# A decoder layer on one core: the MLP's sums all on VectorE, the norm's root applied to the squared activations, another order of the down passes

## The chip, the core and the metric

The kernel runs on one core of a Trainium2 chip. A core has TensorE (matmuls, PE), VectorE (DVE), ScalarE (ACT), GpSimd (POOL) and SyncE (SP, which issues the DMAs). Each engine takes its instructions strictly in the order of its own list; between engines semaphores hold an instruction back until its inputs are there and its buffer is free. The metric is the device time of one execution in microseconds.

## What is computed

One layer of a decoder trunk with two token mixers (a gated DeltaNet and a sparse attention), then an MLP with a squared ReLU. The change lies behind the mixers:

```python
mix = sigmoid(gate_dn) * (o_dn @ w_proj_dn) + sigmoid(gate_nsa) * (o_ns @ w_proj_nsa)
x = x + mix @ w_out
h2 = rmsnorm(x, norm_mlp)          # x * rsqrt(mean(x * x) + 1e-6) * gain
x = x + square(relu(h2 @ w_up)) @ w_down
```

Sequence and model width are 1024, the MLP's inner width is 4096, all float32.

## The kernel before

Everything is held transposed: a tile is 128 features by 512 tokens (128x512), the 1024 tokens being two halves. A float32 matmul is made of three matmuls on fp32r operands: each operand is split in a high part (a copy on ScalarE) and a low part (a subtraction on VectorE, L186 for `split`, L277 for weights in `parts`), and high times high, high times low and low times high are summed in PSUM. So every weight tile costs a DMA, a ScalarE copy and a VectorE subtraction before TensorE can use it.

The stages after the mixers, in the order of the code:

- **Merge** (`ns_merge`, times 1590 to 1679 us): for 8 blocks of features and both halves, the sparse mixer's projection (24 matmuls) is gated and added to the DeltaNet's gated projection. The weights come through `unit` (L280), two loads of 128x4x128 into the ring `wr` of three buffers, which lives in the permanent pool `wp`. `ns_rows` loads the mixer's rows in `a11`. The sum of the two mixers (L1409) is on GpSimd.
- **Output projection** (`out_proj`, 1679 to about 1768 us): 16 blocks (half, c) of 24 matmuls each, in the order (0,0), (1,0), (0,1), (1,1), (0,2), (1,2), then c = 3 to 7 of half 0 and c = 3 to 7 of half 1 (`CB` = 3). Each block's sum x is written to DRAM, squared on ScalarE and added to `sums[half]` (on GpSimd for half 0).
- **Root of the norm** (`root_rows`, L244): eight matmuls with one column (four, each in two passes) put the sums of squares of 512 tokens on partitions, VectorE and GpSimd (`pow`) make 128x4 roots, VectorE spreads them on a diagonal (L252), and one matmul with ones brings them back as 128x512 in PSUM. The first root is taken after block (1,3), the second two products into the up projection.
- **Norm** (`norm_first`, `norm_second`): x times gain times root, one VectorE operation for each of 16 tiles, then the sums of Strassen-Winograd's scheme (B11, B21, T1 to T4, B22), each split in high and low parts (`parts_of`) and held in the big tiles.
- **Up projection** (`up_prep`, `up_mm`, `up_out`, `up_sums`, about 1768 to 2087 us): 16 row blocks n of seven products p (1 to 7) instead of eight. A product is 12 matmuls of 128x512. `weights_of` forms the weight side (a11, a12, a21, a22 and their sums), `up_mm` adds the products in PSUM and on VectorE (L1590, L1594), `up_out` squares the ReLU, and `up_sums` forms four more sums which go to DRAM (`acd`) as right sides for the down projection. Preparation runs `LEAD` = 4 products ahead.
- **Down projection** (`down_load`, `down_prep`, `down_mm`, 2087 to 2401 us): two passes n; in each the seven products p in the order of `turns[n]`, and within each p the eight inner blocks i, accumulated in four PSUM tiles `DP`. The side comes through `bb` and is split in `ah`, `al`. After i = 7 the four tiles are added to the x tiles `X1`. The p = 6 weights are `tmp` = a22 − a11.

Sums not named otherwise went to GpSimd: the helper `sub` (L1450) has GpSimd as its default engine. In `weights_of` that is a21 + a22 at p = 5 and a12 − tmp at p = 6, in `up_prep` and `down_prep` a11 − a21, in `up_sums` the last two. In the first down pass a11 − a21 of inner block e is issued five products into the p = 2 turn, e at a time:

```python
e = q - J - 5
if 0 <= e < J:
    sub(DW[0, e, "a11"], DW[0, e, "a11"], DW[0, e, "a21"])
```

The code gives the instructions; a scheduler in the tile framework sets the order in which each engine's list holds them. So where an instruction stands on its engine is seen from the built program, and rows of it are shown with the change below. Buffers come in rings (pools `pw`, `p5`, `pe`, `pf`, `pg`, `ph`), and a load waits until the ring's oldest buffer has been read.

Of the kernel before, what the change touches and what calls it, by code (L numbers as in the profile page):

```python
# [20 lines left out]
D = 1024  # L21
# [125 lines left out]
def body(ctx: ExitStack, tc: tile.TileContext, A, out):  # L147
# [74 lines left out]
    for half in range(2):  # L222
# [3 lines left out]
        if half == 0:  # L226
            load_consts(cp, 0)
            cp_raw = [wp.tile([128, 4, 128], F32, name="wr", bufs=3) for _ in range(2)]
            for i in range(2):
                SY.dma_start(cp_raw[i], A["w_cp"][0][:, 4 * i:4 * i + 4])  # L230
# [236 lines left out]
    def cmp_hidden(u, i):  # L467
# [3 lines left out]
        w1 = wp.tile([128, 4, 128], F32, name="wr", bufs=3)  # L471
# [444 lines left out]
    def fill_nb(u):  # L916
# [3 lines left out]
        def prep():  # L920
            for kp in range(4):
                wr = wp.tile([128, 2, 256], F32, name="wr", bufs=3)
# [475 lines left out]
    def ns_merge(c, half):  # L1398
# [10 lines left out]
        GP.tensor_tensor(md, md, th, OP.add)  # L1409
# [12 lines left out]
    x1, sums = [[], []], [None, None]  # L1422
# [3 lines left out]
    def out_proj(half, c):  # L1426
# [23 lines left out]
    def sub(o, a, b, eng=None):  # L1450
        (eng or GP).tensor_tensor(o, a, b, OP.subtract)
# [14 lines left out]
    def norm_second(r):  # L1466
        raw = R["raw"]
        R["T2"], R["T3"] = big(True), big(True)
        b12, b22, t = [], [], []

        def head(j):
            b12.append(t512(PL.p5, "b", 4))
            V.scalar_tensor_tensor(b12[j], x1[1][j], cols[:, 8 + j:9 + j], r, op0=OP.mult, op1=OP.mult)
            sub(raw[:, j], b12[j], raw[:, j], V)
            b22.append(t512(PL.p5, "c", 8))
            V.scalar_tensor_tensor(b22[j], x1[1][4 + j], cols[:, 12 + j:13 + j], r, op0=OP.mult, op1=OP.mult)

        def second(j):
            t.append(t512(PL.p5, "c", 8))
            sub(t[j], b22[j], raw[:, j], V)  # L1480
            parts_of("T2", t[j], j)

        head(0)
        for j in range(4):
            if j < 3:
                head(j + 1)
            second(j)
        yield
        for j in range(4):
# [12 lines left out]
        yield

    def weights_of(blocks, p, home):

        a11, a12, a21, a22 = [blocks.get(b) for b in ("a11", "a12", "a21", "a22")]
        if p == 6:
            t = t512(home, "tmp", 2)
            sub(t, a22, a11, V)
# [3 lines left out]
        if p == 5:  # L1513
            GP.tensor_tensor(a21, a21, a22, OP.add)
# [236 lines left out]
```

## Time and profile before

| | |
|---|---|
| Time, median of 3 runs | 2409.52 us (2408.16 to 2412.6) |
| Time of the profiled execution | 2409.07 us |
| Its span | 2407.3 us |
| PE busy | 2339.8 us (97%) |
| DVE busy | 1563.8 us (65%) |
| ACT busy | 1093.4 us (45%) |
| POOL busy | 569.0 us (24%) |

The profile is of one execution by the hardware profiler. The span runs from the first instruction to the last, so 1.8 us of the profiled execution's time lie outside it. Busy times count instructions, not waits. A tile's name in a row is that of the program without its number (`wl<-a,wh` is a low part wl made of a weight tile and its high part); a row of PE with x2 is two matmuls in one record. The releaser in brackets behind an idle time is the instruction that was the last to be waited for.

### The profile page before, as it was taken

How to read it: one execution, taken by the hardware profiler on the slowest of the kernel's cores; microseconds unless marked ns; L12 is line 12 of the kernel's file. 1: busy time of each engine (PE TensorE's matmuls, PEld its weight loads, DVE VectorE, ACT ScalarE, POOL GpSimd, SP SyncE). 2: the span in 40 equal slices, each digit the busy share in tenths (PEclk: the TensorE clock that was granted, in tenths of full speed). 3: DMA queues.
4: the chain of work that ended last, by engine and by line, in shares of the span. 5: the costliest groups of instructions: out<-in, count | busy, mean ns of one | idle time of the engine just before them, and what ended most of it. 6: DMA issues, size and time to landing. Idle time of an engine off the chain costs nothing. (4 is left out here: it accounts for less than half of the span.)

```text
span 2407.3 us, 44378 instructions
## 1 busy us (share of the span) xinstructions
PE 2339.8 (97%) x16673; PEld 1916.8 (80%) x16673; DVE 1563.8 (65%) x3626; ACT 1093.4 (45%) x2258; POOL 569.0 (24%) x473
## 2 busy tenths in 40 slices
PE   7999999999999999999999999999999999989999
PEld 5887878787878887877777777778878888878887
DVE  6766664747484838348877777643397666596785
ACT  4233343434344444227666766532355555534443
POOL 3132321203231423000010111012145444260320
PEclk9999999999999999999999999999999999999999
DMA  5421313131212221237432422164425443566333
GB/s 176 135 65 56 85 43 94 42 91 44 80 50 82 51 77 50 87 116 179 131 115 72 115 89 73 32 225 161 148 83 172 144 149 136 204 232 225 109 126 102
DMA packets 237510, 267.37 MB, mean 111 GB/s; under 512 B 76976, under 2 KB 128496, under 8 KB 237168
## 3 DMA queue, kind: packets, MB, share of 16 engines
q1 hardware_dynamic: 237296, 264.55, 35.2%
q8 instruction: 131, 2.15, 0.4%
q14 instruction: 83, 0.68, 0.1%
HBM read 190.05 MB, written 72.38 MB: 109 GB/s over the span
## 5 line engine op out<-in xcount | busy, mean ns | idle before, releaser
L177 PE MATMUL g<-hh,wh 128*128 128x512 f32 (+1 forms) x816 | 335.4, 411 | 8.2 <-ACT hh L174 7.3
L177 PE MATMUL g<-hl,wh 128*128 128x512 f32 (+1 forms) x816 | 327.4, 401 | 0.1
L177 PE MATMUL g<-hh,wl 128*128 128x512 f32 (+1 forms) x816 | 323.5, 396 | 0.0
L177 PE MATMUL V<-big,wh 128*128 128x512 f32 x768 | 239.4, 392 | 1.6 <-DVE c L1594 1.6
L186 DVE TENSOR_TENSOR wl<-a,wh 128x512 fp32r<-128x512 f32 x192 | 160.6, 838 | 111.0 <-ACT wh L174 110.9
L174 ACT ACTIVATE wh<-wr 128x512 fp32r<-128x512 f32 x210 | 132.1, 630 | 207.1 <-PE g L177 131.4
L174 ACT ACTIVATE wh<-a 128x512 fp32r<-128x512 f32 x192 | 121.1, 631 | 219.6 <-PE V L177 109.5
L1223 DVE CUSTOM_DVE_ANT_0 junk<-S,cst 128x384 f32<-128x384 f32 (+3 forms) x320 | 168.4, 533 | 56.8 <-PE S L177 52.7
L277 DVE TENSOR_TENSOR wl<-wr,wh 128x512 fp32r<-128x512 f32 x178 | 123.6, 698 | 111.9 <-ACT wh L174 108.4
L177 PEld LDWEIGHTS g<-hh,wh 128*128 128x128 f32 (+1 forms) x816 | 153.6, 188 | 36.2 <-ACT hh L174 7.5
L174 ACT ACTIVATE P<-T 128x512 f32<-128x512 f32 x228 | 134.0, 597 | 100.9 <-PE T L177 88.9
L177 PEld LDWEIGHTS g<-hh,wl 128*128 128x128 f32 (+1 forms) x816 | 153.4, 188 | 29.5 <-issue 0.6
L177 PEld LDWEIGHTS g<-hl,wh 128*128 128x128 f32 (+1 forms) x816 | 153.8, 188 | 26.4 <-DVE hl L324 0.8
L177 PEld LDWEIGHTS V<-big,wh 128*128 128x128 f32 x768 | 144.7, 189 | 32.7 <-ACT c L174 1.2
L177 PE MATMUL V<-big,wl 128*128 128x512 f32 x384 | 150.5, 392 | 3.2 <-DVE wl L186 3.2
L177 PE MATMUL g<-wh,hh 128*128 128x256 f32 x512 | 147.4, 288 | 0.0
L177 PE MATMUL g<-wl,hh 128*128 128x256 f32 x512 | 144.8, 283 | 0.0
L177 PE MATMUL g<-wh,hl 128*128 128x256 f32 x512 | 144.8, 283 | 0.0
L1272 POOL TENSOR_TENSOR acc<-acc,bs 128x256 f32<-128x256 f32 x62 | 48.9, 789 | 401.3 <-DVE bs L1270 286.9
L177 PEld LDWEIGHTS o<-vv,P 128*64 128x64 f32 x3648 | 116.0, 138 | 27.1 <-issue 20.4
L177 PE MATMUL o<-vv,P 128*64 128x65 f32 x3648 | 130.1, 225 | 0.0
L177 PE MATMUL S<-ks,qc 96*128 96x384 f32 (+3 forms) x320 | 127.1, 409 | 1.6 <-DVE mx L1223 1.4
(371 smaller groups left out, 5709.1 us busy)
## 6 DMA issues: line engine op xcount, KB each, us to landing
bb<-acd SPq DMA_DIRECT2D x112, 256.0 KB, 2.8
wr<-in_w_dn_dram SPq DMA_DIRECT2D x64, 256.0 KB, 2.9
a<-in_w_u_dram SPq DMA_DIRECT2D x64, 256.0 KB, 3.4
acd<-c SPq DMA_DIRECT2D x64, 256.0 KB, 3.0
a<-in_w_d_dram SPq DMA_DIRECT2D x64, 256.0 KB, 4.9
wr<-in_w_nb_dram SPq DMA_DIRECT2D x32, 256.0 KB, 2.7
wr<-in_w_gt_dram SPq DMA_DIRECT2D x32, 256.0 KB, 2.7
gtd<-fx SPq DMA_DIRECT2D x32, 256.0 KB, 2.2
```

What stands on the lines that cost most here:

```text
L174: return SC.activation(o, i, fn, **kw)
L177: return PE.matmul(o, l, r, start=start, stop=stop, skip_group_check=True)
L186: V.tensor_tensor(lo, src, f(hi), OP.subtract)
L277: V.tensor_tensor(wl, wr, f(wh), OP.subtract)
L1223: V.tensor_tensor_reduce(junk[:, :w], ps[:, :w], mask[:, a:b], 1.0, 3e38, OP.add, OP.min, o)
L1272: adds.tensor_tensor(acc, acc, b, OP.add)
```

## The change

In the code:

- The ring `wr` moves from the permanent pool to `cq`, which is closed at the end of the mixers. After that, `unit` stages its weights in the two buffers `a22` of the pool `pw`.
- Every sum and difference of the stages from the merge on is on VectorE. GpSimd keeps none of them.
- `out_proj` also forms y = x times gain on ScalarE. The sums of half 1 (b12 − B11 and so on) are formed behind each block c of 4 to 7 (`norm_second(j)`), from y, without the root. T2 is split before the up loop, T3, T4, T1 and B22 at its products 2, 4, 6 and 8.
- `root` brings the sum of squares to all partitions with one matmul with ones, then scales it, adds epsilon and takes the reciprocal, all 128x512 on VectorE. The result, one over the mean square, multiplies the squared ReLU in `up_out` (the ReLU is homogeneous, so the root's square can be applied behind the square).
- The first down pass has the order (4, 2, 1, 5, 6, 3, 7); a22 is released at p = 6, a11 − a21 is formed with p = 1, and a22 is the first weight loaded. a21 and a22 now lie in `pg`, a11 and a12 in `ph`.

```diff
     def unit(src):
         ks = []
         for i in range(2):
-            wr = wp.tile([128, 4, 128], F32, name="wr", bufs=3)
+            if hasattr(PL, "pw"):
+                wr = PL.pw.tile([128, 512], F32, name="a22", bufs=2).rearrange("p (a b) -> p a b", a=4)
+            else:
+                wr = PL.cq.tile([128, 4, 128], F32, name="wr", bufs=3)
             SY.dma_start(wr, src[:, 4 * i:4 * i + 4])
...
         V.scalar_tensor_tensor(th, th, 1.0, py, op0=OP.add, op1=OP.mult)
-        GP.tensor_tensor(md, md, th, OP.add)
+        V.tensor_tensor(md, md, th, OP.add)
...
         SY.dma_start(x1d[c, :, HALF[half]], x)
+        if half == 0:
+            y = raw[:, c]
+        else:
+            y = t512(PL.p5, *(("b", 4) if c < 4 else ("c", 8)))
+            (b12 if c < 4 else b22).append(y)
+        act(y, x, AF.Copy, scale=cols[:, 8 + c:9 + c])
...
-            (V if half else GP).tensor_tensor(sums[half], sums[half], sq, OP.add)
+            V.tensor_tensor(sums[half], sums[half], sq, OP.add)
 
     def root(half):
-        return root_rows(sums[half], PL.pq, "Q", PL.pw, PL.p5.tile([128, 4], F32, name="r4", bufs=1), 2)
+        p = t512(PL.pq, "Q")
+        mm(p, K("ones"), sums[half], True, True)
+        rr[half] = r = sums[half]
+        V.tensor_scalar(r, p, 1.0 / D, EPS, op0=OP.mult, op1=OP.add)
+        V.reciprocal(r, r)
...
-    def sub(o, a, b, eng=None):
-        (eng or GP).tensor_tensor(o, a, b, OP.subtract)
+    def sub(o, a, b):
+        V.tensor_tensor(o, a, b, OP.subtract)
...
+    def norm_first():
         R["B11"], R["B21"] = big(True), big(True)
-        for k in range(8):
-            V.scalar_tensor_tensor(raw[:, k], x1[0][k], cols[:, 8 + k:9 + k], r, op0=OP.mult, op1=OP.mult)
-            parts_of("B21" if k >= 4 else "B11", raw[:, k], k % 4)
...
+        parts_of("B11", [raw[:, k] for k in range(4)])
+        parts_of("B21", [raw[:, k] for k in range(4, 8)])
+
+    def norm_second(j):
+        sub(raw[:, j], b12[j], raw[:, j])
+        t2s.append(t512(PL.p5, "u", 4))
+        sub(t2s[j], b22[j], raw[:, j])
+        sub(b12[j], b22[j], b12[j])
+        sub(raw[:, 4 + j], raw[:, 4 + j], t2s[j])
...
         if p == 5:
-            GP.tensor_tensor(a21, a21, a22, OP.add)
+            V.tensor_tensor(a21, a21, a22, OP.add)
...
         act(x, x, AF.Square)
+        r = rr[p in (0, 3)]
+        V.tensor_tensor(x, x, r, OP.mult)
         H[n, p] = x
...
-    turns = [(1, 2, 6, 5, 7, 3, 4), (2, 1, 5, 6, 3, 7, 4)]
+    turns = [(4, 2, 1, 5, 6, 3, 7), (2, 1, 5, 6, 3, 7, 4)]
...
-    LAST = {7: "a11", 3: "a12", 5: "a21", 4: "a22"}
+    LAST = {7: "a11", 3: "a12", 5: "a21", 6: "a22"}
...
-            DW[n, i, b] = t = t512(PL.pg if d == 0 else PL.ph, b, J)
+            DW[n, i, b] = t = t512(PL.pg if m else PL.ph, b, J)
...
-        if n and p == 1:
+        if p == 1:
             sub(w["a11"], w["a11"], w["a21"])
-        e = q - J - 5
-        if 0 <= e < J:
-            sub(DW[0, e, "a11"], DW[0, e, "a11"], DW[0, e, "a21"])
...
         if (half, c) == (1, CB):
-            norm_first(root(0))
+            root(0)
+            norm_first()
+        if half and c >= 4:
+            norm_second(c - 4)
+    norm_parts("T2")
...
-        if q == 2:
-            second = norm_second(root(1))
-        if q in (2, 7, 8):
-            next(second)
+        if q in (2, 4, 6, 8):
+            norm_parts(("T3", "T4", "T1", "B22")[q // 2 - 1])
+        if q == 3:
+            root(1)
```

Three places of the built programs. The first is the start of the merge stage on VectorE. `wl_18987` and `wl_18993` are the low parts of the first w_pn unit, `wl_19064` the first of the second unit; `o_18945` and `o_18949` are the low rows of the two halves; V_19000 is the product of block (0,0). Before:

```order
L277 TENSOR_TENSOR wl_18993<-wr_18990,wh_18992 128x512
L1352 SCALAR_TENSOR_TENSOR th_18891<-th_18891,g_18854 128x512
L186 TENSOR_TENSOR o_18945<-a11_18952,o_18944 128x512
L277 TENSOR_TENSOR wl_19064<-wr_19061,wh_19063 128x512
L186 TENSOR_TENSOR o_18945<-a11_18956,o_18944 128x512
L186 TENSOR_TENSOR o_18945<-a11_18960,o_18944 128x512
L186 TENSOR_TENSOR o_18945<-a11_18964,o_18944 128x512
L277 TENSOR_TENSOR wl_19070<-wr_19067,wh_19069 128x512
L186 TENSOR_TENSOR o_18945<-a11_18968,o_18944 128x512
```

and now, some rows further on:

```order
L186 TENSOR_TENSOR o_18945<-a11_18980,o_18944 128x512
L277 TENSOR_TENSOR wl_18993<-a22_18990,wh_18992 128x512
L186 TENSOR_TENSOR o_18949<-a11_19029,o_18948 128x512
L186 TENSOR_TENSOR o_18949<-a11_19033,o_18948 128x512
L1411 SCALAR_TENSOR_TENSOR a12_18996<-a12_18996,V_19000 128x512
L186 TENSOR_TENSOR o_18949<-a11_19037,o_18948 128x512
L1412 TENSOR_TENSOR a21_18997<-a21_18997,a12_18996 128x512
L186 TENSOR_TENSOR o_18949<-a11_19041,o_18948 128x512
L277 TENSOR_TENSOR wl_19064<-a22_19061,wh_19063 128x512
```

The low part of the second unit stood near the head of the stage, ahead of most `o` rows; now it stands behind the first block's merge (L1411) and its sum (L1412).

The second is the last third of the output projection on VectorE, blocks (1,3) to (1,6). Before, a21_20061 and c_20105 are the sums x of blocks (0,7) and (1,3), wl_20223 and wl_20229 the low parts of the weights of block (1,5), wl_20267 and wl_20273 those of (1,6); the big_20149 rows are scaled blocks of half 0:

```order
L1435 TENSOR_TENSOR a21_20061<-a21_20061,V_20063 128x512
L277 TENSOR_TENSOR wl_20223<-wr_20220,wh_20222 128x512
L277 TENSOR_TENSOR wl_20229<-wr_20226,wh_20228 128x512
L1435 TENSOR_TENSOR c_20105<-c_20105,V_20107 128x512
L241 TENSOR_SCALAR r4_20137<-Q_20138 128x4
L277 TENSOR_TENSOR wl_20267<-wr_20264,wh_20266 128x512
L1443 TENSOR_TENSOR u_19719<-u_19719,tmp_20134 128x512
L252 TENSOR_TENSOR tmp_20145<-cst0_114,r4_20137 128x512
L277 TENSOR_TENSOR wl_20273<-wr_20270,wh_20272 128x512
L1463 SCALAR_TENSOR_TENSOR big_20149<-a12_19659,cols_96,Q_20147 128x512
```

Now c_20120 and c_20188 are the sums of blocks (1,3) and (1,4), wl_20230 the first low part for (1,5); s0 and s1 are the sums of squares:

```order
L1439 TENSOR_TENSOR c_20120<-c_20120,V_20122 128x512
L1466 TENSOR_TENSOR big_20159<-big_19647,big_20159 128x512
L1460 TENSOR_SCALAR s0_19690<-Q_20154 128x512
L1466 TENSOR_TENSOR big_20159<-big_19647,big_20159 128x512
L1453 TENSOR_TENSOR s1_19723<-s1_19723,tmp_20151 128x512
L1461 RECIPROCAL s0_19690<-s0_19690 128x512
L1439 TENSOR_TENSOR c_20188<-c_20188,V_20190 128x512
L277 TENSOR_TENSOR wl_20230<-a22_20227,wh_20229 128x512
L277 TENSOR_TENSOR wl_20236<-a22_20233,wh_20235 128x512
L1466 TENSOR_TENSOR u_20223<-c_20217,big_19647 128x512
```

The low parts of (1,5) stood ahead of the sum of block (1,3), two blocks early; now both stand directly behind the sum of block (1,4), and the reciprocal ahead of that.

The third is p = 6 of the first down pass. Before, GpSimd's list held three sums for each inner block there (a11 − a21, a21 + a22 and a12 − tmp):

```order
L1451 TENSOR_TENSOR a11_22950<-a11_22950,a21_23199 128x512
L1514 TENSOR_TENSOR a21_23199<-a21_23199,a22_23201 128x512
L1451 TENSOR_TENSOR a12_23073<-a12_23073,tmp_23420 128x512
L1451 TENSOR_TENSOR a11_22954<-a11_22954,a21_23225 128x512
L1514 TENSOR_TENSOR a21_23225<-a21_23225,a22_23227 128x512
L1451 TENSOR_TENSOR a12_23075<-a12_23075,tmp_23448 128x512
```

Now VectorE has the difference tmp, the sum for a12 and two low parts for each block:

```order
L1466 TENSOR_TENSOR tmp_24026<-a22_23015,a11_23389 128x512
L1466 TENSOR_TENSOR tmp_24053<-a22_23019,a11_23417 128x512
L1466 TENSOR_TENSOR a12_23171<-a12_23171,tmp_24026 128x512
L186 TENSOR_TENSOR wl_24029<-tmp_24026,wh_24028 128x512
L186 TENSOR_TENSOR al_24034<-bb_23873,ah_24033 128x512
L1466 TENSOR_TENSOR a12_23197<-a12_23197,tmp_24053 128x512
L186 TENSOR_TENSOR wl_24056<-tmp_24053,wh_24055 128x512
L186 TENSOR_TENSOR al_24061<-bb_23900,ah_24060 128x512
L1466 TENSOR_TENSOR tmp_24080<-a22_23021,a11_23443 128x512
L1466 TENSOR_TENSOR a12_23221<-a12_23221,tmp_24080 128x512
```

GpSimd has none of them; the sums a11 − a21 and a21 + a22 stand with p = 1 and p = 5, earlier on VectorE's list.

## Rows read from the trace of the kernel before

**Rows 1.** The page of the whole execution, its first part: busy time, share of the span and instructions of each engine.

```profile
PE 2339.8 (97%) x16673; PEld 1916.8 (80%) x16673; DVE 1563.8 (65%) x3626; ACT 1093.4 (45%) x2258; POOL 569.0 (24%) x473
```

**Rows 2.** The chain of waits from 2160 to 2230 us: start, duration, engine, tile and line, count.

```profile
2185.30 21.76 PE Q L177 x96
```

**Rows 3.** The waits of TensorE from 1560 us to the end: who waited, for what, us in total, times, longest.

```profile
PE Q L177 <- DVE al L186: 6.0, 3, 2.2
PE V L177 <- issue: 4.9, 1, 4.9
PE V L177 <- DVE wl L186: 3.2, 1, 3.2
PE V L177 <- DVE c L1594: 1.6, 2, 0.8
PE Q L177 <- DVE tmp L252: 1.6, 1, 1.6
PE Q L177 <- DVE c L1476: 1.2, 1, 1.2
PE Q L177 <- DVE wl L186: 1.2, 1, 1.2
```

**Rows 4.** Windows of the span: start and end, length, busy time of each engine with its instructions in brackets, granted TensorE clock (1.00 is full), share of the DMA engines, GB/s.

```profile
1587.60:1594.30 6.70, 4.34 (x10) 3.51 (x11) 3.19 (x5) 1.90 (x4) 0.00 (x0) 0.50 0.77 263
1684.00:1769.00 85.00, 85.00 (x379) 70.14 (x378) 41.78 (x66) 30.49 (x49) 14.20 (x10) 1.00 0.45 150
1769.00:1820.00 51.00, 44.17 (x180) 34.44 (x179) 49.31 (x59) 30.26 (x54) 34.06 (x22) 0.93 0.20 67
1795.80:1802.50 6.70, 5.66 (x13) 4.45 (x14) 6.70 (x9) 4.79 (x9) 2.12 (x2) 0.50 0.07 20
1850.00:2050.00 200.00, 200.00 (x884) 165.61 (x883) 127.87 (x148) 112.03 (x188) 82.56 (x52) 1.00 0.43 146
2108.00:2160.00 52.00, 44.83 (x181) 35.54 (x180) 46.03 (x44) 17.72 (x31) 40.78 (x24) 0.93 0.62 218
2140.60:2143.80 3.20, 3.20 (x9) 2.51 (x8) 3.20 (x5) 0.00 (x0) 3.12 (x3) 0.50 0.51 164
2154.20:2157.40 3.20, 3.20 (x9) 2.42 (x9) 3.20 (x3) 1.71 (x4) 2.44 (x2) 0.50 0.27 105
```

**Rows 5.** The timeline of TensorE at four of its waits: start, duration, engine, line, operation, tiles, idle time before and what ended it.

```profile
1796.84 0.79 PE L177 MATMUL V<-big,wl 128*128 128x512 f32 x1 [3.16 <-DVE wl L186]
...
2134.97 0.50 PE L177 MATMUL Q<-al,wh 128*128 128x512 f32 x1 [1.75 <-DVE al L186]
...
2140.22 0.59 PE L177 MATMUL Q<-al,wh 128*128 128x512 f32 x1 [2.23 <-DVE al L186]
...
2152.27 0.49 PE L177 MATMUL Q<-al,wh 128*128 128x512 f32 x1 [2.00 <-DVE al L186]
```

**Rows 6.** The timeline of GpSimd at the begin of p = 6 of the first down pass (same columns).

```profile
2120.23 1.74 POOL L1451 TENSOR_TENSOR a<-a,a 128x512 f32<-128x512 f32 x1
2122.05 1.80 POOL L1514 TENSOR_TENSOR a<-a,a 128x512 f32<-128x512 f32 x1
```

**Rows 7.** The timeline of VectorE in the same stretch.

```profile
2119.04 1.78 DVE L186 TENSOR_TENSOR al<-bb,ah 128x512 fp32r<-128x512 f32 x1
2122.00 0.69 DVE L1451 TENSOR_TENSOR tmp<-a,a 128x512 f32<-128x512 f32 x1 [1.18 <-POOL a L1451]
```

**Rows 8.** The timeline of VectorE at 1802 us, where GpSimd is idle: four subtractions of two SBUF operands, in one row.

```profile
1801.99 2.49 DVE L1451 TENSOR_TENSOR big<-b,big 128x512 fp32r<-128x512 f32 x4
```

**Rows 9.** The groups of VectorE in the steady up stage, 1850 to 2050 us, shapes apart: line, engine, operation, tiles, count, busy us and mean ns of one, idle before and releaser.

```profile
L186 DVE TENSOR_TENSOR wl<-a,wh 128x512 fp32r<-128x512 f32 x63 | 53.9, 856 | 37.3 <-ACT wh L174 37.3
L186 DVE TENSOR_TENSOR wl<-tmp,wh 128x512 fp32r<-128x512 f32 x11 | 19.6, 1785 | 0.0
...
L1594 DVE TENSOR_TENSOR c<-c,V 128x512 f32<-128x512 f32 x11 | 7.4, 675 | 0.0
```

**Rows 10.** The page, its fifth part: groups of instructions by line over the whole span, with busy us and mean ns of one.

```profile
L174 ACT ACTIVATE wh<-wr 128x512 fp32r<-128x512 f32 x210 | 132.1, 630 | 207.1 <-PE g L177 131.4
...
L277 DVE TENSOR_TENSOR wl<-wr,wh 128x512 fp32r<-128x512 f32 x178 | 123.6, 698 | 111.9 <-ACT wh L174 108.4
```

**Rows 11.** The timeline of TensorE at the first root: the eight small matmuls, and the wide one with the diagonal.

```profile
1744.46 0.95 PE L177 MATMUL Q<-cst,u 128*128 128x1 f32 x8
...
1748.37 1.02 PE L177 MATMUL Q<-tmp,cst 128*128 128x512 f32 x2
```

**Rows 12.** The groups of VectorE over the whole span: the reciprocals.

```profile
L1266 DVE RECIPROCAL coef<-o 128x4 f32<-128x4 f32 x64 | 11.5, 180 | 51.3 <-PE o L177 51.0
...
L419 DVE RECIPROCAL s<-s 128x64 f32<-128x64 f32 x1 | 0.5, 546 | 0.0
```

**Rows 13.** The issues of SyncE at the start of the merge stage, four of them in one row.

```profile
1590.30 3.03 SPq L1395 DMA_DIRECT2D a<-ond  x4
```

**Rows 14.** The DMA issues of the whole span: tensors, count, KB of each, median us from issue to landing.

```profile
a<-in_w_d_dram SPq DMA_DIRECT2D x64, 256.0 KB, 4.9
...
wr<-in_w_o_dram SPq DMA_DIRECT2D x26, 256.0 KB, 2.9
...
wr<-in_w_pn_dram SPq DMA_DIRECT2D x16, 256.0 KB, 3.7
```

**Rows 15.** The timeline of VectorE at the first merge.

```profile
1597.78 0.69 DVE L1408 SCALAR_TENSOR_TENSOR a<-a,V 128x512 f32<-128x512 f32 x1 [1.46 <-PE V L177]
```

More of the change, by code (lines that the diff above doesn't have):

```diff
@@ L227, in body @@
             load_consts(cp, 0)
-            cp_raw = [wp.tile([128, 4, 128], F32, name="wr", bufs=3) for _ in range(2)]
+            cp_raw = [PL.cq.tile([128, 4, 128], F32, name="wr", bufs=3) for _ in range(2)]
             for i in range(2):
@@ L470, in cmp_hidden @@
         x = CX["x", u]
-        w1 = wp.tile([128, 4, 128], F32, name="wr", bufs=3)
+        w1 = PL.cq.tile([128, 4, 128], F32, name="wr", bufs=3)
         SY.dma_start(w1, A["cw1"][v, i])
@@ L921, in prep @@
             for kp in range(4):
-                wr = wp.tile([128, 2, 256], F32, name="wr", bufs=3)
+                wr = PL.cq.tile([128, 2, 256], F32, name="wr", bufs=3)
                 SY.dma_start(wr, A["w_nb"][u, kp])
@@ L1420, in body @@
     pool("p5")
-    x1, sums = [[], []], [None, None]
+    x1, sums, rr = [[], []], [None, None], [None, None]
+    raw, b12, b22, t2s = f(big(False)), [], [], []
     CB = 3
@@ L1436, in out_proj @@
         SY.dma_start(x1d[c, :, HALF[half]], x)
+        if half == 0:
[4 more added lines that the diff above has]
+        act(y, x, AF.Copy, scale=cols[:, 8 + c:9 + c])
         if c == 0:
-            sums[half] = t512(PL.p5, "u", 4)
+            sums[half] = t512(PL.p5, f"s{half}", 1)
             act(sums[half], x, AF.Square)
@@ new lines, in root, with parts_of @@
+        p = t512(PL.pq, "Q")
[5 more added lines that the diff above has]
+        V.tensor_tensor(o, a, b, OP.subtract)
+    R = {}
+    def parts_of(n, srcs, i0=0):
+        for i, src in enumerate(srcs):
+            act(R[n][:, i0 + i], src)
+            sub(R[n][:, i0 + 4 + i], src, f(R[n][:, i0 + i]))
+    def norm_first():
+        R["B11"], R["B21"] = big(True), big(True)
+        parts_of("B11", [raw[:, k] for k in range(4)])
+        parts_of("B21", [raw[:, k] for k in range(4, 8)])
@@ L1504, in weights_of, with norm_parts @@
+    def norm_second(j):
[4 more added lines that the diff above has]
+        sub(raw[:, 4 + j], raw[:, 4 + j], t2s[j])
+    def norm_parts(n):
+        R[n] = big(n in ("T2", "T3"))
+        parts_of(n, {"T2": t2s, "T3": b12, "T4": [raw[:, 4 + j] for j in range(4)],
+                     "T1": [raw[:, j] for j in range(4)], "B22": b22}[n])
     def weights_of(blocks, p, home):
@@ L1508, in weights_of @@
             t = t512(home, "tmp", 2)
-            sub(t, a22, a11, V)
+            sub(t, a22, a11)
             src = t
@@ L1679, in down_loads @@
             if q % 2:
-                x_load(q // 2, 0)
+                x_load(4 + q // 2, 0)
         elif q < 16:
+            down_load(0, q - 8, "a11")
             down_load(0, q - 8, "a21")
-            down_load(0, q - 8, "a22")
+            if q % 2:
+                x_load(q // 2 - 4, 0)
         elif q < 24:
-            x_load(q - 16, 1)
-        elif q < 28:
-            x_load(q - 20, 0)
+            x_load((q - 12) % 8, 1)
     def x_load(c, h):
@@ L1716, in body @@
             for i in range(J):
-                down_load(0, i, "a11")
+                down_load(0, i, "a22")
                 if i < RING:
```

43 lines of the change are left out of this document (2 added, 41 removed).

## The prediction

> **What bounds the kernel now.** I read the busy shares first. TensorE computes 97% of the span and VectorE 65%, GpSimd 24% [rows 1]: only what lets TensorE wait, slows its clock or lengthens its own list can move the time. A product of the MLP stage is 12 matmuls; 96 take 21.76 us in the chain [rows 2], so one is 0.227 us, a product 2.72 us, and a row block of the output projection (24) 5.44 us. Nothing in the change alters these.
>
> Second, what TensorE waits for from 1560 us on [rows 3]. Two places hold nearly all that the change can reach. At the start of the up projection: 1.6 (the diagonal for the root), 1.2 (a normalised block), 3.2 (a low weight part) and one of the two 0.8 at L1594, 6.8 us in all. In the first down pass: 6.0 for `al` and 1.2 for `wl`, 7.2 us. The 4.9 at the start of the merge stage isn't touched: that product's PSUM tile needs the last DeltaNet gate, as before.
>
> Third, the granted clock [rows 4]. It is 0.50 (1.2 GHz in place of 2.4) in three stretches right behind these waits: 6.70 us with 5.66 of matmuls behind the 3.16 us wait at 1796.84 [rows 5], and twice 3.20 us, full of matmuls, behind those of 2.23 and 2.00 us. At full clock the same work takes half, so the clock costs 2.8 + 1.6 + 1.6 = 6.0 us.
>
> Fourth, why VectorE is late there. In the down pass with p = 6, GpSimd has three sums for each inner block at 1.74 to 1.80 us apiece [rows 6], 5.3 us against the product's 2.72. VectorE waits for GpSimd, and its own subtractions of two SBUF operands take 1.78 us where they meet a running sum of GpSimd's, 0.69 where they start in a gap between two [rows 7]. With GpSimd idle four run in 2.49 us, one every 0.605 [rows 8]. The steady up stage shows both kinds mixed: a mean of 856 ns for `wl<-a`, 1785 for `wl<-tmp`, yet 675 where one operand lies in PSUM [rows 9]. So GpSimd is the culprit twice, as a slow producer and as a neighbour.
>
> **The change, part by part.** All against the profiled execution: 2409.07 us (the median of the runs is 0.45 above it).
>
> *Sums to VectorE.* In the first down pass this removes the producer that could not keep up. VectorE's list with p = 6 becomes four operations per block and four sums into x: 36 x 0.605 = 21.8 us against 8 x 2.72 = 21.76, level, with a lead of four products in hand; p = 1 and p = 5 have 28 operations (16.9 us). So the 7.2 us of waits and their 3.2 us of clock go: −10.4. In the up stage one n has 14 VectorE operations now and gets five from GpSimd and four multiplications: 23 x 0.605 = 13.9 of 19.04 us. That fits, and no wait of TensorE is there to be won: the whole stretch 1850 to 2050 is full [rows 4].
>
> *Norm parts beside the output projection, 1/ms after the square.* The chain root, diagonal, second matmul, eight scaled blocks, low parts no longer stands between the last projection block and the first products: only T2's parts do, and the factors come from ScalarE (16 more there at about 0.63 us [rows 10], against 30.49 busy in the 85 us of the projection [rows 4]; hidden). The four waits of 6.8 us go with their 2.8 us of clock: −9.6. Of root 0 the eight small matmuls go, 0.95 us on a busy TensorE; the wide one stays [rows 11]: −0.95. Root 1's eight I take at nothing (bounds 0 and −0.95), since what ends there afterwards is new. The 64 multiplications are in the 23 above; uncovered they would cost 64 x 0.605 = 39 us.
>
> *Reciprocal of 128x512.* The trace has it only small: 180 ns for 4 columns, 546 for 64 [rows 12]. Their slope (6.1 ns a column) gives 3.3 us, plain proportion to the second 4.4. I take 3.3, the two rows' line. One stands in the last third of the projection, the other beside the first products.
>
> The Trainium skill (VectorE: DVE Perf Modes, section "First, the fixed hardware budget") says that Reciprocal is an iterative divide with a repeat count of 8; at the page's 0.96 GHz this makes an estimate of 512 x 8 / 0.96 = 4.3 us. The rows' slope is below that; by the page the forecast would be 1 us later.
>
> *New wait A, merge stage.* With the `wr` ring gone from the permanent pool, w_pn can't be fetched before `pw` opens. The second unit's load (a22_19061) stands on SyncE behind four `a<-ond` issues that end at 1593.3 [rows 13]; 3.7 us to land [rows 14] and 0.63 on ScalarE give 1597.7. Its low part then stands on VectorE behind the first merge: L1411 (at 1597.78 before, [rows 15]), an `o` row, the sum taken over from GpSimd and another `o` row, so it ends at 1597.78 + 4 x 0.605 + 0.69 = 1600.9. TensorE finishes block (0,0) at about 1597.6 and has seven matmuls left (1.6 us) that don't need it: 1599.2. Wait 1.7 us; 0.5 if the load comes with the `a<-ond` rows, 3.5 if the merge waits for `mxd`.
>
> *New wait B, projection block (1,5).* Its first low part now stands on VectorE behind the sum of (1,4), which waits for TensorE's last matmul of that block. With nothing else queued this costs 0.6 + 0.7 less the two matmuls of cover (0.45): 0.9 us. Behind the sum of (1,3) stand four short operations and the reciprocal, 5 x 0.605 + 3.3 = 6.3 us in a block of 5.44, so 0.9 us of backlog are added: 1.8 us. Bounds 0.9 and 3.0 (reciprocal of 4.4).
>
> *New wait C, start of the up projection.* VectorE is the full engine there (49.31 of 51 us busy before [rows 4]). Following its new rows at 0.605 us each, each not before its ScalarE copy or its product, the low part for (1,1) comes 0.9 us late, that for (0,6) 0.6, and (0,3), which overwrites a PSUM tile still to be read by the sum of (0,5), waits 1.4: 2.9 us. Bounds 0 (it keeps pace as in the steady stage) and 6.8 (as now).
>
> *Clock behind the new waits.* The waits of 1.2 and the 1.75 us at 2134.97 kept the full clock, 2.23 lowered it, and so did 2.00 with a 1.2 close behind [rows 3 to 5]. The new ones are mostly shorter; I take 0.9 us, one drop of 1.6 with a chance of about one in two, bounds 0 and 8.
>
> *Weight stream.* A slot of `a22` is taken for landing 2.9 us [rows 14], 0.63 copy and 0.70 low part [rows 10]: 4.2 us, while TensorE uses up both slots in 5.44. Hidden; the third slot is not missed. *Turn order, a22 loaded first:* p = 4 needs one weight and one side, so p = 6 comes fifth and finds its a11 − a21 long done. Nothing on the path by itself, 0; without the sums' move it would only shift the wait.
>
> **Sum.** −10.4 − 9.6 − 0.95 = −21.0; + 1.7 + 1.8 + 2.9 + 0.9 = +7.3; net −13.7. 2409.07 − 13.7 = 2395.4, **2395 us**, own range 2391 to 2400.
>
> **Rivals.**
> *The new waits don't open* (SyncE further ahead than the old rows show, VectorE idle at the right moment; it was only 41.78 of 85 us busy in the projection [rows 4]): 2388. Against it: the positions in the list are plain.
> *Each new wait lowers the clock*: three drops of 2.8 and the upper half of the bounds, +8.4 + 3: 2402 to 2407, around the edge of faster. For it: wait A follows soon on a stretch at 0.50 [rows 4]. Against: 1.75 did not suffice [rows 5].
> *The down gain fails*: if VectorE's 1.78 is not GpSimd's doing but the loads' (this stretch moves 218 GB/s against 146 in the up stage [rows 4]), p = 6 takes 36 x 1.7 = 61 us and waits far more; if only some are slow, the wait stays as it is, +10.4: 2406, no change. Against: the 0.69 at 2122.00 stands among the same loads [rows 7].
> *The weight stream starves, slower*: with two slots and a landing of 4.9 as that of `a<-in_w_d` [rows 14], the cycle is 4.9 + 0.63 + 0.70 = 6.2, and with each low part behind the preceding block's sum (as B) 1.3 more, 7.5: 2.1 us late for each of the ten blocks with a unit of their own, +21: 2416. It decides from a cycle of 6.8 us, 1.4 late per block. Against: landing 2.9, and only (1,5) has its first low part behind the preceding sum; in two others it is the second, with 14 matmuls (3.2 us) of cover.
>
> **How the numbers follow.** The measurement can tell about 0.2%, 4.8 us, from no change: faster is below 2404.7. Forecast 0.60; no new waits 0.12; reciprocal by the longer bound (2396 to 2397) 0.05; clock rival 0.10, half of it each side of 2404.7; down gain fails 0.06; stream starves 0.07. Faster 0.60 + 0.12 + 0.05 + 0.05 = 0.82; within 0.05 + 0.06 = 0.11; slower 0.07. The range takes in the cases from 2387 to 2405.
>
> **What would show it.** Right: the page's GpSimd line without the MLP's sums, VectorE's low parts near 0.69 throughout, no `al` or `wl` wait of TensorE between 2100 and 2160, waits of 1 to 2 us behind `wl` at the start of the merge and in projection block (1,5). Wrong: RECIPROCAL above 4.4 us, low parts still at 1.78 with GpSimd idle, a wait for `wh` or `a22` in every projection block, half clock in more stretches than now.

## The result and the profile after

The changed kernel takes 2389.99 us (median of 4, 2388.08 to 2391.49) against 2409.17 us of the kernel before (median of 4, 2408.16 to 2412.6): ratio 0.9917, 95% interval 0.99 to 0.9935. So it is 19 us faster, where 14 were forecast. Its profiled span is 2386.3 us, 21.0 less than before.

The first part of the page [rows 1]: GpSimd's time is almost halved, VectorE's grows by only 37 us, though it has 211 operations more (64 of them the multiplications by one over the mean square).

```profile
PE 2330.9 (98%) x16657; PEld 1910.6 (80%) x16657; DVE 1601.1 (67%) x3837; ACT 1101.7 (46%) x2274; POOL 304.7 (13%) x308
```

The waits of TensorE from 1560 us on (who, for what, us in total, times, longest), to be laid beside [rows 3]:

```profile
PE V L177 <- ACT o L174: 4.3, 1, 4.3
PE V L177 <- DVE wl L277: 1.5, 2, 0.9
PE Q L177 <- DVE wl L186: 1.3, 2, 0.9
PE V L177 <- DVE c L1585: 0.8, 1, 0.8
PE g L177 <- DVE th L1355: 0.8, 1, 0.8
PE V L177 <- ACT wh L174: 0.8, 1, 0.8
PE Q L177 <- ACT wh L174: 0.5, 1, 0.5
PE Q L177 <- ACT b L174: 0.2, 1, 0.2
```

No `al` is waited for any more. The `wl` of L277 are waits A and B of the prediction, the `wh` for V is another part of A, and the three rows for Q are wait C. Not new are `c` and `th`, 0.8 each, which the kernel before has too. The places of A, B and the first of C, in the timeline of TensorE (start, duration, tiles, idle before and releaser):

```profile
1596.07 1.20 PE L177 MATMUL V<-o,wh 128*128 128x512 f32 x4 [0.77 <-ACT wh L174]
...
1598.49 0.50 PE L177 MATMUL V<-o,wl 128*128 128x512 f32 x1 [0.54 <-DVE wl L277]
...
1751.78 0.50 PE L177 MATMUL V<-big,wl 128*128 128x512 f32 x1 [0.93 <-DVE wl L277]
...
1775.66 0.50 PE L177 MATMUL Q<-big,wl 128*128 128x512 f32 x1 [0.92 <-DVE wl L186]
```

The windows that answer to [rows 4] (busy time and count of PE, PEld, DVE, ACT, POOL, clock, DMA share, GB/s): the start of the up stage, its steady part, and the first turns of the down pass.

```profile
1769.00:1820.00 51.00, 48.96 (x211) 38.91 (x210) 50.87 (x80) 30.61 (x57) 0.00 (x0) 1.00 0.28 99
1850.00:2050.00 200.00, 200.00 (x884) 165.62 (x883) 154.59 (x242) 112.90 (x190) 0.00 (x0) 1.00 0.38 138
2099.00:2151.00 52.00, 52.00 (x231) 43.07 (x230) 43.88 (x72) 23.08 (x40) 0.00 (x0) 1.00 0.92 327
```

The clock is full in all three. In the steady part VectorE does 242 operations in 154.59 us where it did 148 in 127.87. Three of its groups there, to be laid beside [rows 9], are a low part, a difference of two SBUF tiles and the new multiplication (L1542); each takes 0.69 us now.

```profile
L186 DVE TENSOR_TENSOR wl<-a,wh 128x512 fp32r<-128x512 f32 x63 | 43.3, 687 | 3.8 <-ACT wh L174 3.8
...
L1542 DVE TENSOR_TENSOR b<-b,s 128x512 f32<-128x512 f32 x11 | 7.6, 693 | 0.4
...
L1466 DVE TENSOR_TENSOR u<-b,u 128x512 f32<-128x512 f32 x11 | 7.6, 692 | 0.4
```

The same difference in the same window of the kernel before took 1.67 us:

```profile
L1451 DVE TENSOR_TENSOR u<-b,u 128x512 f32<-128x512 f32 x11 | 18.3, 1667 | 2.9 <-ACT b L174 2.9
```

The two wide reciprocals of the whole span, to be laid beside [rows 12], take 3.35 us:

```profile
L1461 DVE RECIPROCAL s<-s 128x512 f32<-128x512 f32 x2 | 6.7, 3350 | 0.0
```

Where the time came from is best read by stages: the start of the first matmul of each, and the end of the last, from the timeline of TensorE. Before: last gate product ended 1585.10, merge 1589.96, projection 1679.18, up 1768.05, down 2086.59, end 2403.45. After: 1583.71, 1588.03, 1678.63, 1767.82, 2077.63, 2382.43. The differences, with the same for the experiments:

| run | gap + merge | projection | up | down | stages together |
|---|---|---|---|---|---|
| before | 94.08 | 88.87 | 318.54 | 316.86 | 818.35 |
| changed | 94.92 | 89.19 | 309.81 | 304.80 | 798.72 |
| e1 down weight sums on GpSimd | 94.29 | 89.19 | 309.47 | 307.65 | 800.60 |
| e2 sums only | 93.70 | 88.88 | 318.83 | 304.80 | 806.21 |
| e3 turn order only | 93.04 | 88.87 | 319.80 | 307.63 | 809.34 |
| e4 useless GpSimd sums | 94.51 | 89.18 | 309.70 | 318.34 | 811.73 |
| e5 no multiplication | 94.16 | 89.20 | 308.49 | 304.81 | 796.66 |
| e6 early units | 94.80 | 89.18 | 309.80 | 304.80 | 798.58 |
| e7 rest on GpSimd | 97.21 | 93.14 | 323.77 | 304.80 | 818.92 |
| e8 tuned | 95.04 | projection and up 395.85 | | 304.80 | 795.69 |
| e9 wr kept, two buffers | 95.48 | 89.24 | 310.14 | 304.80 | 799.66 |
| e10 tuned, wr kept | 92.98 | projection and up 395.88 | | 304.81 | 793.67 |

The stages of the change give 19.63 us, which agrees with the medians (19.2). The other 1.4 us of the two spans is the mixers', where only the pool of the ring `wr` differs: over these runs (e9 and e10 left out) their end lies between 1583.2 and 1591.5 us. So a single execution's total says less than its stages. These repeat within 0.4 us in the kernels that share the changed code of a stage (projection 89.18 to 89.20, up 309.47 to 309.81, down 304.80). The up stage in its old form, with long waits and half-clock stretches, repeats less well: 318.54 before and 319.80 in e3, whose edit doesn't touch its start.

### The profile page after: what moved, and what is told of

Its sections match the earlier page's. It is cut to its first block, busy times and chain, and to the rows that moved or that the text cites. A ratio compares the mean times of both kernels' runs of the same rounds, so it can differ in the third digit from the quotient of the medians.

```text
span 2386.3 us, 44222 instructions
## 1 busy us (share of the span) xinstructions
PE 2330.9 (98%) x16657; PEld 1910.6 (80%) x16657; DVE 1601.1 (67%) x3837; ACT 1101.7 (46%) x2274; POOL 304.7 (13%) x308
## 4 chain that ended last, share of the span: by engine, by line
PE 84%; DVE 8%; DMA 3%; POOL 2%; issue 2%; ACT 1%; SPq 0%; DVEq 0%; POOLq 0%; ACTq 0%
PE g L177 29%; PE V L177 20%; PE Q L177 12%; PE T L177 5%; PE o L177 5%; PE s L177 4%; PE c L177 3%; PE S L177 3%; PE m L177 1%; DVE acc L676 1%; DMA ab<-asc 1%; DVE St L849 1%; PE tp L609 0%; POOL sa L337 0%; PE m L1280 0%
## 5 line engine op out<-in xcount | busy, mean ns | idle before, releaser
L174 ACT ACTIVATE wh<-a 128x512 fp32r<-128x512 f32 x234 | 146.7, 629 | 248.2 <-PE V L177 153.9
L186 DVE TENSOR_TENSOR wl<-a,wh 128x512 fp32r<-128x512 f32 x192 | 132.0, 689 | 74.3 <-ACT wh L174 74.2
L174 ACT ACTIVATE wh<-wr 128x512 fp32r<-128x512 f32 x168 | 105.5, 629 | 157.2 <-PE g L177 127.7
L277 DVE TENSOR_TENSOR wl<-wr,wh 128x512 fp32r<-128x512 f32 x136 | 94.7, 701 | 90.3 <-ACT wh L174 89.3
L676 DVE SCALAR_TENSOR_TENSOR acc<-xp,cols,acc 128x512 f32<-128x512 f32 x144 | 117.0, 813 | 6.2 <-ACT acc L174 4.8
```

Source lines behind the costliest of these rows:

```text
L174: return SC.activation(o, i, fn, **kw)
L186: V.tensor_tensor(lo, src, f(hi), OP.subtract)
L277: V.tensor_tensor(wl, wr, f(wh), OP.subtract)
L676: V.scalar_tensor_tensor(a2, xp[:, i:i + 512], cols[:, c0 + i:c0 + i + 1], a2, op0=OP.mult, op1=OP.add)
```

## Experiments

**e1: the down projection's weight sums back on GpSimd**, new order kept (`down` is true for the down projection's weights alone).

```diff
+        E = GP if down else V
         if p == 5:
-            V.tensor_tensor(a21, a21, a22, OP.add)
+            E.tensor_tensor(a21, a21, a22, OP.add)
...
-            sub(a12, a12, t)
+            E.tensor_tensor(a12, a12, t, OP.subtract)
...
         if p == 1:
-            sub(w["a11"], w["a11"], w["a21"])
+            GP.tensor_tensor(w["a11"], w["a11"], w["a21"], OP.subtract)
```

> The changed kernel with the three weight sums of the down projection (a11 - a21, a21 + a22, a12 - tmp) back on GpSimd; turn order and all else as changed. Theory of the prediction, the engine decides: TensorE's waits for al and wl in the first pass come back, 8 to 12 us slower than the changed kernel (2398 to 2402). Rival, the order decides: in the new order the three sums belong to three different turns (p = 1, 5, 6), one of 1.8 us per product of 2.72, so GpSimd keeps up and the time stays within 2 us of the changed kernel (2390 to 2392), though VectorE's low parts go back to a mix of 0.69 and 1.78 us.

Measured: 2394.85 us, ratio to before 0.9939 (0.9924 to 0.9954). The total is between the two, but the mixers of its profiled execution ended 6.1 us later than the changed kernel's; the stage says 307.65 against 304.80. Only 2.85 us of the 12.06 come back, so the rival, that the order decides, is nearer. The place shows something about reading waits, too (timeline of TensorE):

```profile
2137.25 0.39 PE L177 MATMUL Q<-ah,wl 128*128 128x512 f32 x1
2137.48 0.39 PE L177 MATMUL Q<-ah,wh 128*128 128x512 f32 x1
2138.25 0.50 PE L177 MATMUL Q<-al,wh 128*128 128x512 f32 x1 [0.39 <-DVE al L186]
2138.59 0.39 PE L177 MATMUL Q<-ah,wl 128*128 128x512 f32 x1
2138.82 0.40 PE L177 MATMUL Q<-ah,wh 128*128 128x512 f32 x1
```

Matmuls start every 0.227 us, while one is drawn 0.39 us long. The idle of 0.39 us stands for 2138.25 − 2137.48 − 0.227 = 0.54 us, and the next spacing is 0.34 in place of 0.227: 0.65 us in all, 0.26 more than the bracket (the idle time that the row gives). Below, "by the starts" means a wait counted in this way: what the spacings of the matmuls' starts exceed 0.227 us by.

**e2: the kernel before with all sums on VectorE, nothing else.**

```diff
-        (eng or GP).tensor_tensor(o, a, b, OP.subtract)
+        V.tensor_tensor(o, a, b, OP.subtract)
...
-            GP.tensor_tensor(a21, a21, a22, OP.add)
+            V.tensor_tensor(a21, a21, a22, OP.add)
```

(and the same for the sums in the merge and of the squares)

> The kernel before with all sums of merge, norm, up and down on VectorE, and nothing else changed (old norm chain, old turn order, old w_pn staging). Theory, the engine decides: the 12 us of the first down pass are gained, while the start of the up projection keeps most of its 9 us, since the chain of the root remains and VectorE gets 22 more operations there: 2395 to 2400. Rival, the order decides: the old order still puts three weight sums in one turn, now with 5 to 6 VectorE operations per product (6 x 0.605 = 3.6 us against 2.72), so a wait for al remains and 2402 to 2408 comes out.

Measured: 2395.91 us, ratio 0.9945 (0.9926 to 0.9964). Down 304.80, as in the changed kernel: with the old turn order VectorE alone removes all 12.06 us. Up 318.83, no gain at all. The theory holds, and the rival's `al` wait doesn't appear.

**e3: the kernel before with the new turn order and its loads only.**

```diff
-    turns = [(1, 2, 6, 5, 7, 3, 4), (2, 1, 5, 6, 3, 7, 4)]
+    turns = [(4, 2, 1, 5, 6, 3, 7), (2, 1, 5, 6, 3, 7, 4)]
...
-    LAST = {7: "a11", 3: "a12", 5: "a21", 4: "a22"}
+    LAST = {7: "a11", 3: "a12", 5: "a21", 6: "a22"}
```

(and a11 − a21 formed with p = 1, with the loads and pools that the new order needs)

> The kernel before with the new turn order and its loads alone; all sums stay on GpSimd and the norm chain stays. Theory of the prediction: 0 (the wait is only shifted), 2406 to 2412. Rival, the order decides: the three GpSimd sums are spread over three turns as in the second pass of the kernel before, which has a wait of only 0.23 us; then the 12 us of the first pass are gained by the order alone, 2396 to 2400.

Measured: 2402.65 us, ratio 0.9964 (0.9952 to 0.9975). Down is 307.63: the order alone gains 9.23 of the 12.06 us, and the theory of the prediction fails here. The stage says more than the total, since the profiled execution's up stage was 1.26 us longer than before and its mixers ended 3.3 us later. The waits of this kernel from 1560 us on:

```profile
PE V L177 <- DVE wl L186: 3.2, 1, 3.2
PE V L177 <- DVE c L1594: 2.4, 2, 1.6
PE Q L177 <- DVE tmp L252: 2.0, 1, 2.0
PE Q L177 <- DVE al L186: 1.2, 3, 0.4
```

The `al` of 6.0 us [rows 3] is down to 1.2, with GpSimd as slow as before. Its timeline shows how:

```profile
2134.68 1.73 POOL L1451 TENSOR_TENSOR a<-a,a 128x512 f32<-128x512 f32 x1
2136.49 1.62 POOL L1514 TENSOR_TENSOR a<-a,a 128x512 f32<-128x512 f32 x1
2138.07 1.75 POOL L1451 TENSOR_TENSOR a<-a,a 128x512 f32<-128x512 f32 x1
...
2171.26 1.29 POOL L1451 TENSOR_TENSOR a<-a,tmp 128x512 f32<-128x512 f32 x1 [16.05 <-DVE tmp L1451]
```

It now has the pair a11 − a21 and a21 + a22 for each block, 3.4 us against the product's 2.72, and after the first two blocks the third sum (`a<-a,tmp`) only after a pause of 16 us; before, it had all three together for five blocks (the first two sums of one in [rows 6]). So it isn't one sum per turn, as the rival of e1 had it, but two at once; that the overload is now small enough for the lead of four products is the likely reading, not tested by itself.

**e4: useless GpSimd sums beside p = 6 in the changed kernel.**

```diff
+        if p == 6:
+            for _ in range(3):
+                du = t512(PL.ph, "du", 1)
+                GP.tensor_tensor(du, w["a12"], w["a11"], OP.add)
         if p in LAST:
```

> The changed kernel with three GpSimd additions of two SBUF tiles (a12 + a11, into a tile that nobody reads) behind each block of p = 6 in both down passes; nothing waits for their results. It adds work whose result isn't used. Theory, GpSimd is also a neighbour that slows VectorE: VectorE's sums of two SBUF operands go to 1.78 us while these run (5.3 us per product of 2.72, so through p = 6 and the next turn), 36 x 1.7 = 61 us in a turn of 21.8, TensorE waits 10 to 30 us per pass, 2410 to 2450. Rival, only the producer counted: VectorE stays at 0.69 and the time within 2 us of the changed kernel.

Measured: 2402.1 us, ratio 0.9972 (0.9959 to 0.9985). Down goes from 304.80 to 318.34, +13.54 us for work that nobody waits for. The groups of VectorE in a p = 6 turn of it, 2164 to 2190 us (in the changed kernel `al<-bb` takes 687 ns on the mean there):

```profile
L186 DVE TENSOR_TENSOR al<-bb,ah 128x512 fp32r<-128x512 f32 x6 | 8.4, 1403 | 0.0
L1466 DVE TENSOR_TENSOR a<-a,tmp 128x512 f32<-128x512 f32 x4 | 5.8, 1446 | 0.1
L186 DVE TENSOR_TENSOR wl<-tmp,wh 128x512 fp32r<-128x512 f32 x5 | 5.7, 1130 | 0.0
...
L1656 DVE TENSOR_TENSOR x<-x,V 128x512 f32<-128x512 f32 x4 | 2.5, 672 | 0.0
```

Operations of two SBUF tiles are stretched, the one that reads PSUM is not, and VectorE waits for no other engine in this stretch. So GpSimd's part as a neighbour is shown. The means of 1.13 to 1.45 us are less than the 1.78 that the expectation put on each, and the price, 6.8 us a pass, is below the 10 to 30 expected.

**e5: without the 64 multiplications.**

```diff
-        r = rr[p in (0, 3)]
-        V.tensor_tensor(x, x, r, OP.mult)
         H[n, p] = x
```

> The changed kernel without the multiplication of the squared activations by one over the mean square (64 VectorE operations left out, so its output lacks the norm). Theory: they are hidden in the steady up stage; from the first up product to the first down matmul it takes as long as the changed kernel (309.8 us), at most 1 us less at the start, where VectorE is full; down 304.8. Rival: VectorE sets the pace of the up stage at 23 operations, then up to 39 us less.

This kernel leaves out the norm's factor, so it computes something else and only its time is of use. Measured: 2390.41 us in a single execution; up 308.49 against 309.81. So the multiplications cost 1.3 us, a little over the 1 us that was allowed for, all at the start of the up stage (the waits of 0.48 and 0.41 us there are gone), and nothing in the steady part.

**e6: the first two weight units of the merge stage asked for ahead of the rows.**

```diff
+    ks[0] = unit(A["w_pn"][0])
     ns_rows(0)
+    ks[1] = unit(A["w_pn"][1])
```

> The changed kernel with the first two weight units of the merge stage asked for ahead of the rows of the halves, nothing else. Theory: wait A is an effect of the load's place on SyncE's list and of the low part's place behind the merge; the merge stage goes from 90.6 to about 89.3 us, total 1 to 2 us less than the changed kernel. Rival: the rows, which now land later, take the wait over: the gap ahead of the first merge matmul grows by as much, total within 0.5 us.

Measured: 2389.92 us, ratio 0.9908 (0.9887 to 0.9928), as the changed kernel. Both of A's waits are gone from the merge, and stand ahead of it (timeline of TensorE; 4.32 us in the changed kernel):

```profile
1590.59 1.19 PE L177 MATMUL V<-o,wh 128*128 128x512 f32 x2 [5.53 <-ACT o L174]
```

The rival holds: gap and merge together are 94.80 against 94.92, since the gap grew from 4.32 to 5.53 us.

**e7: the sums of merge, projection, norm and up back on GpSimd**, with the new norm chain; down stays on VectorE.

```diff
-        sub(b12[j], b22[j], b12[j])
-        sub(raw[:, 4 + j], raw[:, 4 + j], t2s[j])
+        gsub(b12[j], b22[j], b12[j])
+        gsub(raw[:, 4 + j], raw[:, 4 + j], t2s[j])
...
-        sub(b12, b22, b12)
-        sub(b21, b21, t)
+        gsub(b12, b22, b12)
+        gsub(b21, b21, t)
```

(gsub is `sub` on GpSimd; the sums of the weights, of B22's low parts, of half 0's squares and of the merge likewise)

> The changed kernel with the sums of the merge, the projection, the norm and the up projection back on GpSimd where they were before; the new norm chain stays, and the down projection stays all on VectorE. Theory, GpSimd as a neighbour costs where VectorE is full: the start of the up projection loses 2 to 8 us of its 8.7 (312 to 318 us from first up product to first down matmul), the steady part nothing, down 304.8. Rival: the shape of the norm chain alone made the gain, 309 to 311 us.

Measured: 2410.45 us in a single execution, as slow as the kernel before although its down stage has the full gain. Up 323.77, which is 5.2 us longer than before, projection +4.3, gap and merge +3.1. Its waits from 1560 us on:

```profile
PE Q L177 <- ACT b L174: 5.3, 1, 5.3
PE V L177 <- DVE wl L277: 3.9, 3, 1.9
...
PE Q L177 <- DVE s L1453: 3.3, 1, 3.3
PE Q L177 <- DVE wl L186: 2.1, 1, 2.1
```

Both views fail: the shape of the norm chain alone doesn't make the gain, and the loss is beyond the 8 us expected at most: the up stage is 14.0 us longer than the changed kernel's. At 1780 to 1820 us `wl<-a` takes 1239 ns on the mean there, so GpSimd slows VectorE in this stretch. How much of the loss is that, and how much is GpSimd being late with its own sums, this run doesn't separate.

**e8: places on VectorE's list.** e6's early units; each projection unit created one block ahead; T2 to B22 split one product later, the second root at product 9.

```diff
-        if q in (2, 4, 6, 8):
-            norm_parts(("T3", "T4", "T1", "B22")[q // 2 - 1])
-        if q == 3:
+        if q in (1, 3, 5, 7, 9):
+            norm_parts(("T2", "T3", "T4", "T1", "B22")[q // 2])
+        if q == 9:
             root(1)
```

> The changed kernel with the early units of the merge stage, each projection unit asked for one block ahead (so that its low parts stand ahead of the preceding sum on VectorE), T2 to B22 split one up product later and the second root six products later. Theory: waits A, B and C were effects of places on VectorE's list: merge 89.3, projection 88.2, up about 308 us; 3 to 5 us less than the changed kernel (2385 to 2387). Rival: the load moves on, other products wait in turn (T2's parts now close to their first use), total within 1 us of the changed kernel.

Measured: 2387.78 us, ratio 0.9901 (0.9886 to 0.9917), 2.2 us below the changed kernel's median; the intervals overlap, so the totals don't separate the two. The stages do: projection and up together 395.85 against 399.00. B is down to 0.23 us, of C one wait of 0.23 us is left:

```profile
PE V L177 <- issue: 5.9, 1, 5.9
...
PE Q L177 <- ACT b L174: 0.2, 1, 0.2
PE V L177 <- DVE wl L277: 0.2, 1, 0.2
```

The gain is 3.15 us in these stages, near the 396 us that the expectation gives, and none at the merge, where A only moved and 89.3 had been expected.

**e9 and e10: the ring `wr` back in the permanent pool, with two buffers for all its users**; e9 is the changed kernel with it, e10 the tuned one (without the early units).

```diff
-            if hasattr(PL, "pw"):
-                wr = PL.pw.tile([128, 512], F32, name="a22", bufs=2).rearrange("p (a b) -> p a b", a=4)
-            else:
-                wr = PL.cq.tile([128, 4, 128], F32, name="wr", bufs=3)
+            wr = wp.tile([128, 4, 128], F32, name="wr", bufs=2)
```

> The changed kernel with the ring wr back in the permanent pool for all its users, but with two buffers in place of three (three don't fit beside the two tiles for the sums of squares). Theory: wait A was the price of the ring's move, since with a persistent ring the first w_pn tiles are fetched before the merge stage; merge about 89.3 us in place of 90.6, and the gap ahead of it not longer than 4.9, so 1 to 2 us less than the changed kernel. Rival: the gap is set by the rows and the last gate alone and the saving is given back there, as with the early units; within 0.5 us.

> The tuned kernel (projection units one block ahead, T2 to B22 split one product later, second root at product 9) with the ring wr in the permanent pool with two buffers in place of the early units. Theory: its waits B and C stay away (projection and up together about 396 us) and wait A goes as well, merge 89.3 and gap 4.3 to 4.9: 3 to 4.5 us less than the changed kernel. Rival: two buffers of wr hold the mixers or the projection back, within 1 us of the tuned kernel.

Measured: 2399.64 us (ratio 0.9953, 0.9937 to 0.9969) and 2396.92 us (0.9947, 0.9932 to 0.9963): slower than the changed kernel by about 10 and 7 us. Both views of e9 fail, and e10's rival holds in kind but costs far more than 1 us. The loss lies in the mixers, which end at 1594.0 and 1596.9 us; they use the same ring. With two buffers TensorE waits longer there (waits of e9 over the whole span; in the changed kernel the loads cost 1.1 and `cx` 0.9), which accounts for 6.1 us:

```profile
PE g L177 <- DVE cx L355: 4.7, 3, 2.1
...
PE s L177 <- DMA wr<-in_cw_dram: 3.4, 3, 1.9
```

Gap and merge are 95.48 in e9 and 92.98 in e10, so what keeping the ring would be worth is not settled by them. From the runs with three buffers in the permanent pool (before, e2, e3: 93.04 to 94.08) and those without (changed, e1, e4 to e6: 94.16 to 94.92) it is somewhat below 1 us; this is an estimate, since those kernels differ in other things too.

## Why the prediction held, and where its steps failed

The sign and the places were right, and the time lies in the wide range of 2387 to 2405. The forecast was 5 us short, and the measured 2389.99 us lies 1 us below the prediction's own range of 2391 to 2400. By the number alone the rival that the new waits don't open (2388) came nearer, but they did open: by the starts they cost 6.2 us, against 6.4 forecast. What the prediction had too small is the gain.

- **Down, −10.4: −12.06 measured.** The mechanism was right and the term too small. The three waits for `al`, the `wl` and a last one of 0.2 us were taken at their brackets; by e1's reading each is 0.26 us more, 5 x 0.26 = 1.3 us, which with the 0.2 left out makes 11.9.
- **"Turn order ... nothing on the path by itself, 0; without the sums' move it would only shift the wait": wrong.** e3 gives 9.23 us for the order alone, e2 12.06 for the sums alone; together 12.06. Either cure works, and they don't add. The kernel before had the hint in its own second pass, where the order was already of this kind and `al` shows a wait of 0.2 us.
- **"GpSimd is the culprit twice": shown for the neighbour, by e4.** For the producer the trace of the kernel before has VectorE idle for GpSimd from 2112 to 2156 us:

```profile
DVE tmp L1451 <- POOL a L1451: 4.7, 4, 1.2
```

  The shares of the two in the 12.06 us are not shown, since e1 to e3 move both together. The rival that loads stretch VectorE's operations is refuted: the changed kernel moves 327 GB/s at 2099 to 2151 us, and its group there is

```profile
L186 DVE TENSOR_TENSOR al<-bb,ah 128x512 fp32r<-128x512 f32 x22 | 15.2, 690 | 0.5 <-ACT ah L174 0.5
```

- **Start of the up stage, −9.6 + 2.9 + 0.9 = −5.8: −8.73 measured.** By the starts, the four old waits with their clock cost 10.9 us, not 9.6. Wait C cost 3.1 (brackets 0.92 + 0.48 + 0.41 + 0.23 = 2.0), near the 2.9, but in part by luck: (1,1) and (0,6) cost 1.2 and 1.4 in place of 0.9 and 0.6, (0,7) cost 0.5 that was not forecast, and the 1.4 at (0,3) never opened. No clock drop followed. Root 1's eight small matmuls, taken at nothing, held TensorE for 0.81 us in the kernel before, and the spacing behind them was 0.1 longer than usual:

```profile
1773.49 0.95 PE L177 MATMUL Q<-cst,u 128*128 128x1 f32 x8
1774.30 0.72 PE L177 MATMUL V<-big,wh 128*128 128x512 f32 x2
```

  So −10.9 − 0.9 + 3.1 = −8.7. The reason failed, too: the step credits the gain to the norm chain alone and lists the sums' move under the down pass only. The four cases are 318.54 (neither), 318.83 (sums, e2), 323.77 (chain with sums on GpSimd, e7), 309.81 (both). So the chain pays only together with the sums' move. The likely reason is that it loads VectorE more in the very stretch where it is full (80 operations at 1769 to 1820 us in place of 59), which it can bear only when GpSimd doesn't slow it; that is argued from e7's rows, not tested apart.
- **Multiplications "in the 23 above"**: hidden in the steady stage, but 1.3 us at the start (e5).
- **Reciprocal 3.3 us: 3.35 measured.** The line through the two small rows was right. The estimate of 4.3 us from the Trainium skill (VectorE: DVE Perf Modes, section "First, the fixed hardware budget") was 0.9 us too long; the measurement decides.
- **Wait A, 1.7 us: 1.85 by the starts** (brackets 0.77 + 0.54). The low part stood behind the first merge as forecast, but 1.0 of it was a wait for the ScalarE copy `wh`, which the prediction had in time. What the idle time ahead of the merge and the half-clock stretch behind it cost came out 1.0 us smaller (the granted clock was 0.50 for 3.4 us in place of 6.7 [rows 4]). The prediction has no term for that, and it is of the size by which gap and merge vary among before, e2 and e3. So gap and merge lost 0.84 in all. e6 shows that A is not free to be won: the loads in front only change places.
- **Wait B, 1.8 us: 1.2 by the starts** (bracket 0.93). Less 0.9 for root 0's small matmuls this is the 0.32 us by which the projection got longer, where 0.85 were forecast. VectorE's timeline there (sum of (1,3), then reciprocal, sum of (1,4), both low parts of (1,5)) shows that the reciprocal made no backlog: it ended 6.3 us after the start of (1,3)'s sum, as reckoned, but TensorE's wide matmul for the root (drawn 1.0 us) lies between the two blocks, so that (1,4)'s sum began 6.3 us later too, not 5.44:

```profile
1744.12 0.69 DVE L1439 TENSOR_TENSOR c<-c,V 128x512 f32<-128x512 f32 x1
...
1747.13 3.35 DVE L1461 RECIPROCAL s<-s 128x512 f32<-128x512 f32 x1
1750.43 0.69 DVE L1439 TENSOR_TENSOR c<-c,V 128x512 f32<-128x512 f32 x1
1751.04 1.29 DVE L277 TENSOR_TENSOR wl<-a,wh 128x512 fp32r<-128x512 f32 x2
```

- **Clock, 0.9 us: none.** The changed kernel's waits behind the start of the merge, all below 1 us by their brackets, lowered it nowhere.

In sum the forecast missed by 1.7 us in the down pass, 2.9 in the up stage and 1.4 in merge and projection, all to the same side. The old waits were worth 3 us more than their brackets and clock, root 1's matmuls 0.9 more than nothing, the clock and B came out 0.9 and 0.6 below their terms, and the start of the merge gave 1.0; A and C came out 0.3 above theirs.

## What to carry to other kernels

A sum given to GpSimd to spare VectorE can cost twice: here it took up to 1.8 us in place of 0.69, and while it ran VectorE's own operations on two SBUF tiles stretched (e4); check in the trace whether the slow ones meet a running GpSimd sum before VectorE is called full. Two cures of the same wait don't add, and a rearrangement that loads an engine more may pay only behind the change that frees it: test parts alone and together. Where the profile's early part varies by microseconds from run to run, compare stages by their first matmuls.

## What was not expected of the hardware

Three GpSimd sums per block that nobody reads cost 13.5 us in two passes (e4), while VectorE waited for no engine; its operations that read PSUM were spared. A bracket of idle time at TensorE understates a wait by 0.26 us here (0.39 drawn, 0.65 lost), since matmuls are drawn 0.39 us long at a spacing of 0.227.
